# VectorE takes over GpSimd's arithmetic in the fast matrix products of a hybrid encoder layer

## The chip, the core and the metric

The kernel runs on one core of a Trainium2 chip. The core has a matrix engine (TensorE, PE in the profile), three engines for elementwise work (VectorE is DVE, ScalarE is ACT, GpSimd is POOL), SBUF for tiles of 128 partitions, and PSUM, where TensorE writes and from which VectorE and ScalarE read. All DMAs of this kernel are issued from one queue, SyncE's (SP). The metric is the time of one execution on the device in microseconds; smaller is better.

## What is computed

One layer of a residual block, 1024 real tokens and 16 meta tokens, width 1024. Two mixers (a gated delta rule and a stick-breaking attention) work on one input projection; their outputs are projected, gated, merged and projected again, and a SwiGLU feed-forward network (FFN) follows. All of it is float32. The part that matters here, shortened:

```python
D_MODEL, SEQ, D_FF = 1024, 1024, 2816
def hybrid_mixer(hn, ..., w_branch_dn, w_branch_sb, w_out):
    ...                                   # o_dn: T x 2048, o_sb: T x 1024
    merged = jax.nn.sigmoid(gate_dn) * (o_dn @ w_branch_dn) + jax.nn.sigmoid(gate_sb) * (o_sb @ w_branch_sb)
    return merged @ w_out
def swiglu(hn, w_ffn_in, w_ffn_out):
    gate, up = jnp.split(hn @ w_ffn_in, 2, axis=-1)
    return (jax.nn.silu(gate) * up) @ w_ffn_out
# per layer
h = h + hybrid_mixer(rmsnorm(h, norm_mix_gain[l]), ...)
h = h + swiglu(rmsnorm(h, norm_ffn_gain[l]), w_ffn_in[l], w_ffn_out[l])
```

## The kernel before

**Precision.** A float32 operand is cut into a high part (ScalarE casts it to the matrix engine's format) and a low part (a subtraction, the source minus the high part), and each product is three matmuls: high with high, high with low, low with high. The cut of an activation block is `split2` (tiles `b` and `t`, two casts and two subtractions of 128x1024 for a block); the cut of a weight is `w_split` (tile `ws`, one cast and one subtraction of 128x512).

**The fast product.** From the second half of the branch projection on, matrix products are done two by two blocks at a time in the Strassen-Winograd way: seven block products in place of eight, paid for with additions of operand blocks and of results. `wino_steps` does one: `A` holds the weight quadrants (tiles `w`, `wr`, `s`, `stg`), `B` the activation quadrants (`x`, `b`, `b11r`, `mg`). It issues the products in the order 1, 2, 6, 7, 4, 5, 3. `stage` runs one product as four quarters `p`; a quarter is one `w_split`, twelve matmuls of 128x512 (nine in the last group of the FFN) into one PSUM bank, and an `evac` that reads the bank. `bop` adds or subtracts activation quadrants, `aop` weight quadrants, two instructions of 128x1024 each. Of ten such pairs, five are given the engine `gx`, which is GpSimd; the others run on VectorE.

**Where it runs.** In this order: the second half of the delta-rule branch (evacuation `accumulate` into `mg`, and `gate_dn`, which multiplies by a gate tile `gt`); the stick-breaking branch (`sb_evac`, which adds gated results to `mg`); the output projection (`accumulate` into `h2`, with `h2_final` summing squares into `ssq` for the norm); and, after the first FFN projection, three groups of the second FFN projection (`accumulate` into `h3`, tile `h` in the trace). Between them lies the first FFN projection, 22 steps of `ffn_a` (two products with `b11`, `b21`) and `ffn_b` (five products with `t1`, `t2`, `b22`, `t3`, `t4`, with weight sums made by `comb` on GpSimd). Its entry norms the four quadrants and makes t1, t2, t3, t4 and b22 out of them (`each`); from tile `rows`, a ScalarE copy of the norm's PSUM row, GpSimd scales quadrant 22. Products 5 and 6 of `ffn_b` use different PSUM banks (`pb`, `pa`), and a ScalarE copy of each follows.

**What sets the order.** Tile pools hand out buffers and semaphores order their reuse. Each engine runs its own instructions strictly in the order in which the program has them, and waits at the first one that isn't ready. The order here is made when the program is built, by a scheduler that goes by a timeline of its own, so that moving an instruction to another engine, or writing it elsewhere, also moves others. All elementwise helpers (`sub`, `add`, `mul`) have one line each, L1116, L1119 and L1122; rows are told apart by the tiles.

Of the kernel before, what the change touches and what calls it, by code (L numbers as in the profile page):

```python
# [9 lines left out]
F32 = mybir.dt.float32  # L10
# [5 lines left out]
P = 128  # L16
# [24 lines left out]
def build(tc, ctx, hT, w_mix, w_ab, w_bd, w_bs, w_o, w_fi, w_fo, small, adt, outT):  # L41
    nc = tc.nc
# [1075 lines left out]
    def add(out, a, b, eng=None):  # L1118
        (eng or nc.vector).tensor_tensor(out, a, b, op=ALU.add)  # L1119

    def mul(out, a, b, eng=None):
        (eng or nc.vector).tensor_tensor(out, a, b, op=ALU.mult)  # L1122
# [5 lines left out]
    def ent(ts, k):  # L1128
        return ts[k // 2][:, k % 2]
# [21 lines left out]
    def w_split(src):  # L1151

        n = src.shape[1]
        wsn[0] += 1
        t = wp.tile([P, KT, P], R32, tag=("wh", "wl")[wsn[0] % 2], name="ws")
        hi, lo_ = t[:, 0:n], t[:, 4:4 + n]
        nc.scalar.copy(hi, src)  # L1157
        sub(lo_, src, hi.bitcast(F32))
        return hi, lo_

    def mmw(ps, w, b, kh, more=False):

        n = 3 * kh
        i = 0
        for k in range(kh):
            bh, bl = (t[:, k % 2] for t in b[k // 2])
            for (x, y) in ((w[0][:, k], bh), (w[0][:, k], bl), (w[1][:, k], bh)):
                nc.tensor.matmul(ps, x, y, start=(i == 0 and not more), stop=(i == n - 1),  # L1168
                                 skip_group_check=more)
                i += 1  # L1170
# [74 lines left out]
    def wino_steps(kh, B, A, evac, s2=None):  # L1245

        gx = nc.gpsimd
        X, Y = {}, {}  # L1250

        def stage(name, ws, b, acc, more=False):
            for p in range(4):
                w = w_split(ent(ws, p)[:, 0:kh * P].rearrange("p (k c) -> p k c", c=P))
                if not more:
                    acc[p] = bank("pa" if acc is X else "pb", p)
                mmw(acc[p], w, b, kh, more)
                evac(name, p, acc[p])

        def bop(f, o, a, b, eng=None):  # L1260
            for i in range(2):
                n = min(2, kh - 2 * i)
                f(B[o][i][:, :n], B[a][i][:, :n], B[b][i][:, :n], eng)

        def aop(f, o, a, b, eng=None):
            for x, y, z in zip(o, a, b):
                f(x[:, :, 0:kh * P], y[:, :, 0:kh * P], z[:, :, 0:kh * P], eng)

        b11 = split_of(B["11"], kh, "b")
        stage("1", A["11"], b11, X)  # L1270
        yield
        b21 = split_of(B["21"], kh, "b")
        stage("2", A["12"], b21, Y)
        yield
        bop(sub, "11", "12", "11")
        bop(sub, "11", "22", "11")
        t2 = split_of(B["11"], kh, "b")
        s2 = s2 or [wp.tile([P, KT, P], F32, tag="wr", name="s2").rearrange("p (a k) c -> p a (k c)", a=2)
              for i in range(2)]
        aop(sub, A["11"], A["11"], A["21"], gx)  # L1280
        aop(sub, s2, A["22"], A["11"])
        stage("6", s2, t2, X, True)
        bop(sub, "21", "21", "11", gx)
        bop(sub, "12", "22", "12", gx)
        bop(sub, "11", "22", "11")
        aop(add, A["21"], A["21"], A["22"], gx)
        aop(sub, A["12"], A["12"], s2, gx)
        t3 = split_of(B["12"], kh, "b")
        stage("7", A["11"], t3, X, True)
        t4 = split_of(B["21"], kh, "b")  # L1290
        stage("4", A["22"], t4, X, True)
        t1 = split_of(B["11"], kh, "b")
        b22 = split_of(B["22"], kh, "b")
        stage("5", A["21"], t1, Y)
        stage("3", A["12"], b22, Y, True)
# [21 lines left out]
    def gate(j, q, p):  # L1317
        r, hs = quad(q)
        g_ = late["g"]()
        nc.sync.dma_start(g_, gate_d[j * KT + r + p, :, hs])  # L1320
        return g_

    def gate_dn(q, p):
        c = ent(mg[q], p)
        mul(c, c, gate(0, q, p), nc.gpsimd if q == "21" else None)

    def sb_evac(u):

        v = []

        def gated(q, p, t, eng=None):
            mul(t, t, gate(1, q, p), eng)
            c = ent(mg[q], p)
            add(c, c, t, nc.gpsimd)

        def tmp():
            return late["g"]()

        def evac(name, p, ps):
            up = ent(u, p)  # L1340
            if name == "1":
                nc.scalar.copy(up, ps)
            elif name == "2":
                t = tmp()
                add(t, up, ps)
                gated("11", p, t)
            elif name == "6":
                nc.scalar.copy(up, ps)
            elif name == "7":
                if p % 2 == 0:  # L1350
                    v.append(v4(wp.tile([P, KT, P], F32, tag="wr", name="v").rearrange("p k c -> p (k c)")))
                nc.scalar.copy(ent(v, p), ps)
            elif name == "4":
                t = gate(1, "21", p)
                mul(t, t, ps)
                c = ent(mg["21"], p)
                add(c, c, t, nc.gpsimd)
            elif name == "5":
                add(ent(v, p), ent(v, p), ps)
                gated("22", p, ent(v, p))  # L1360
            else:
                add(up, up, ps)
                gated("12", p, up)

        return evac
# [41 lines left out]
    lh, lh_st = pool("lh", 1)  # L1407
    ssq = [lh.tile([P, 512], F32, name=f"ssq{i}") for i in range(2)]
    started = [False, False]
    h2 = {}  # L1410
# [7 lines left out]
    def h2_final(q, p):  # L1418
        r, hs = quad(q)
        i = int(q[1]) - 1  # L1420
        c = ent(h2[q], p)
        nc.sync.dma_start(h2_d[r + p, :, hs], c)
        if not started[i]:
            started[i] = True
            nc.scalar.activation(ssq[i], c, AF.Square)
        else:
            sq = lh.tile([P, 512], F32, name="sq2", bufs=1)
            nc.scalar.activation(sq, c, AF.Square)
            add(ssq[i], ssq[i], sq, nc.vector if p == 3 and q != "11" else nc.gpsimd)

    def norm2_sum(i):
        pss = bank(("pa", "pb")[i])
# [37 lines left out]
    def product(w, b, tag="pb"):  # L1470
        ps = bank(tag)
        mmw(ps, w, b, 4)
        return ps
# [29 lines left out]
    def ffn_b(f):  # L1503
        raw, ac, px = fst.pop(f)
        rg, ru = raw or raw_pair(f)
        h0, h1 = HS

        def comb(op, a, b):
            r = fw.tile([P, 4, P], F32, tag="sc", name="sc", bufs=3)
            nc.gpsimd.tensor_tensor(r, a, b, op=op)  # L1510
            return r

        def gate(hs, v):
            nc.scalar.activation(v, ac[:, hs], AF.Sigmoid)
            mul(ac[:, hs], ac[:, hs], v)

        a11, a12, a21, a22 = rg[:, 0:4], rg[:, 4:8], ru[:, 0:4], ru[:, 4:8]
        s1 = comb(ALU.add, a21, a22)
        w5 = w_split(s1)
        s2 = comb(ALU.subtract, s1, a11)  # L1520
        w6 = w_split(s2)
        s4 = comb(ALU.subtract, a12, s2)
        w3 = w_split(s4)
        yield
        u, v, v2 = uv[0][:, f % 2], uv[1][:, 0], uv[1][:, 1]
        gate(h0, v)
        mmw(px, w6, t2, 4, True)
        nc.scalar.copy(u, px)
        py = product(w5, t1)
        nc.scalar.copy(v, py)  # L1530
        mmw(py, w3, b22, 4, True)
        add(ac[:, h1], u, py)
        gate(h1, v2)
        s3 = comb(ALU.subtract, a11, a21)
        mmw(px, w_split(s3), t3, 4, True)
        add(v, v, px)
        mul(ac[:, h1], ac[:, h1], v)
        mmw(px, w_split(a22), t4, 4, True)
        mul(ac[:, h0], ac[:, h0], px)
        nc.sync.dma_start(act_d[f], ac)  # L1540
# [3 lines left out]
    t1, t2 = sblock(slab, "t1"), sblock(slab, "t2")  # L1544
# [1 line left out]
    r2 = norm2_sum(1)  # L1546
    ffn_a(1)
    row = norm2_row(r2, 1)
    rows = lh.tile([P, 512], F32, name="rows")
    nc.scalar.copy(rows, row)  # L1550
    norm2_scale("12", row)


    def each(f, o, a, b, dst, eng=None):
        for i in range(2):
            if f:
                f(h2[o][i], h2[a][i], h2[b][i], eng)
            split2(dst, i, h2[o][i], eng)

    each(sub, "11", "12", "11", t1)  # L1560
    for k in range(4):
        mul(ent(h2["22"], k), ent(h2["22"], k), rows, nc.gpsimd)
    for f in range(2, LEAD):
        ffn_a(f)
    for st in (lh_st, lp_st):
# [2 lines left out]
    b22, t3, t4 = sblock(sl3, "b22"), sblock(sl3, "t3"), sblock(sl3, "t4")  # L1568
    fb = ffn_b(0)
    next(fb)  # L1570

    each(None, "22", None, None, b22, nc.gpsimd)
    each(sub, "11", "22", "11", t2)
    each(sub, "21", "21", "11", t4)
    each(sub, "12", "22", "12", t3, nc.gpsimd)
    uv = [xt(4), xt(5)]

    XW = (-1, -1)
# [106 lines left out]
```

## Time and profile before

| | us |
|---|---|
| time, median of 3 runs | 2661.07 (2660.76 to 2661.66) |
| the profiled execution, its own time | 2659.11 |
| its span | 2657.4 |
| TensorE busy | 2538.1 (96%) |
| VectorE busy | 1637.1 (62%) |
| ScalarE busy | 1085.6 (41%) |
| GpSimd busy | 611.7 (23%) |

Busy shares are means over stages that differ. The changed code runs from about 1655 us to the end of the span, and in it stretches in which TensorE never stops stand beside stretches in which it waits; so the trace is read stretch by stretch. A row of the timeline gives the start, the time that the instruction took, and in brackets how long its engine stood idle before it and what released it. Two instructions of one engine overlap by some 0.07 us, so the cost of one on a full engine is the step from its start to the next one's, a little less than its duration.

### The profile page before, as it was taken

How to read it: one execution, taken by the hardware profiler on the slowest of the kernel's cores; microseconds unless marked ns; L12 is line 12 of the kernel's file. 1: busy time of each engine (PE TensorE's matmuls, PEld its weight loads, DVE VectorE, ACT ScalarE, POOL GpSimd, SP SyncE). 2: the span in 40 equal slices, each digit the busy share in tenths (PEclk: the TensorE clock that was granted, in tenths of full speed). 3: DMA queues.
4: the chain of work that ended last, by engine and by line, in shares of the span. 5: the costliest groups of instructions: out<-in, count | busy, mean ns of one | idle time of the engine just before them, and what ended most of it. 6: DMA issues, size and time to landing. Idle time of an engine off the chain costs nothing.

```text
span 2657.4 us, 40031 instructions
## 1 busy us (share of the span) xinstructions
PE 2538.1 (96%) x15877; PEld 2167.3 (82%) x15877; DVE 1637.1 (62%) x2481; ACT 1085.6 (41%) x2195; POOL 611.7 (23%) x649
## 2 busy tenths in 40 slices
PE   8999999999999999999999999879887999997999
PEld 5788887899999998999989988668676888885777
DVE  5356555346665664455545554997977555557997
ACT  5454444233333333454544554334343333342332
POOL 4011110000111111111111110444545333235221
PEclk9999999999999999999999999999997999998999
DMA  3373554532233332212121133435122222225321
GB/s 107 106 182 123 145 177 131 147 94 76 94 104 104 102 106 72 68 33 64 33 69 59 49 124 103 155 106 174 52 75 95 103 88 81 79 86 176 111 87 64
DMA packets 136440, 265.97 MB, mean 100 GB/s; under 512 B 11564, under 2 KB 55100, under 8 KB 135228
## 3 DMA queue, kind: packets, MB, share of 16 engines
q1 hardware_dynamic: 136252, 263.40, 31.3%
q8 instruction: 125, 2.05, 0.3%
q14 instruction: 63, 0.52, 0.1%
HBM read 196.50 MB, written 66.86 MB: 99 GB/s over the span
## 4 chain that ended last, share of the span: by engine, by line
PE 78%; DVE 12%; DMA 4%; issue 4%; ACT 2%; POOL 1%; SPq 0%; DVEq 0%; ACTq 0%; POOLq 0%
PE pj L108 35%; PE pa L1168 15%; PE pb L1168 10%; DVE b L1116 2%; DVE ws L1116 2%; PE pch L108 2%; DMA zs_d<-gt 2%; PE pout L1083 2%; PE ptr L1068 1%; DVE x L1116 1%; PE pout L765 1%; PE pch L754 1%; PE pout L766 1%; PE pch L760 1%; PE ptr L705 1%
## 5 line engine op out<-in xcount | busy, mean ns | idle before, releaser
L108 PE MATMUL pj<-xh,wh 128*128 128x512 f32 (+5 forms) x1600 | 579.2, 362 | 6.6 <-DVE gt L802 4.8
L108 PE MATMUL pj<-xh,wl 128*128 128x512 f32 (+5 forms) x1600 | 575.8, 360 | 0.0
L108 PE MATMUL pj<-xl,wh 128*128 128x512 f32 (+5 forms) x1600 | 571.4, 357 | 0.6 <-issue 0.6
L108 PEld LDWEIGHTS pj<-xh,wh 128*128 128x128 f32 x1600 | 303.7, 190 | 42.6 <-issue 5.4
L108 PEld LDWEIGHTS pj<-xh,wl 128*128 128x128 f32 x1600 | 303.7, 190 | 29.8 <-issue 1.0
L108 PEld LDWEIGHTS pj<-xl,wh 128*128 128x128 f32 x1600 | 304.0, 190 | 27.6
L1168 PE MATMUL pa<-b,ws 128*128 128x512 f32 x1176 | 287.6, 401 | 34.2 <-DVE h L1119 17.1
L1168 PE MATMUL pb<-b,ws 128*128 128x512 f32 x1212 | 298.4, 397 | 10.3 <-DVE ws L1116 7.7
L1168 PEld LDWEIGHTS pa<-b,ws 128*128 128x128 f32 x1176 | 224.2, 192 | 91.2 <-issue 26.6
L1168 PEld LDWEIGHTS pb<-b,ws 128*128 128x128 f32 x1212 | 229.1, 190 | 66.3 <-DVE ws L1116 11.1
L1168 PE MATMUL pa<-t,ws 128*128 128x512 f32 x792 | 195.3, 396 | 11.9 <-DVE t L1116 11.3
L1168 PEld LDWEIGHTS pa<-t,ws 128*128 128x128 f32 x792 | 150.4, 190 | 47.1 <-DVE t L1116 12.7
L296 DVE SCALAR_TENSOR_TENSOR y<-pj,sm,y 128x346 f32<-128x346 f32 (+2 forms) x216 | 119.1, 572 | 28.5 <-ACT y L292 26.1
L1116 DVE TENSOR_TENSOR ws<-wr,ws 128x512 fp32r<-128x512 f32 x90 | 80.2, 892 | 66.4 <-ACT ws L1157 66.4
L1059 DVE TENSOR_TENSOR_SCAN kpt<-kpt 128x144 f32<-128x144 f32 (+3 forms) x64 | 89.0, 1391 | 49.3 <-POOL kpt L1056 48.4
L921 DVE TENSOR_TENSOR wtl<-ptr,wth 128x512 fp32r<-128x512 f32 (+2 forms) x96 | 52.2, 552 | 101.8 <-ACT wth L920 101.6
L1510 POOL TENSOR_TENSOR sc<-wr 128x512 f32<-128x512 f32 x44 | 67.4, 1532 | 176.9 <-DVE ws L1116 170.8
L1157 ACT CAST ws<-sc 128x512 fp32r<-128x512 f32 x88 | 52.9, 620 | 123.6 <-PE pa L1168 108.9
L1054 POOL TENSOR_SCALAR_AFFINE_SELECT spt<-spt 128x128 f32<-128x128 f32 x64 | 26.7, 417 | 274.0 <-ACT spt L1051 262.7
L800 ACT ACTIVATE gt<-pj 128x512 f32<-128x512 f32 x48 | 28.6, 596 | 144.2 <-PE pj L108 97.8
L100 DVE TENSOR_TENSOR wl<-wr,wh 128x1024 fp32r<-128x1024 f32 x46 | 56.3, 1223 | 47.8 <-ACT wh L99 47.8
L108 PE MATMUL pj<-wh,xh 128*128 128x256 f32 (+1 forms) x288 | 83.7, 291 | 0.0
(431 smaller groups left out, 5028.9 us busy)
## 6 DMA issues: line engine op xcount, KB each, us to landing
wr<-in_w_mix_dram SPq DMA_DIRECT2D x80, 512.0 KB
wr<-in_w_fi_dram SPq DMA_DIRECT2D x48, 512.0 KB
act_d<-ac SPq DMA_DIRECT2D x22, 512.0 KB
lrep<-ld SPq DMA_DIRECT2D x64, 144.0 KB
zs_d<-gt SPq DMA_DIRECT2D x32, 256.0 KB
gate_d<-gt SPq DMA_DIRECT2D x32, 256.0 KB
zt<-zs_d SPq DMA_DIRECT2D x32, 256.0 KB
odn_d<-zt SPq DMA_DIRECT2D x32, 256.0 KB
```

Source lines behind the costliest of these rows:

```text
L100: (eng or nc.vector).tensor_tensor(wl, wr, wh.bitcast(F32), op=ALU.subtract)
L108: nc.tensor.matmul(ps, u, v, start=(i == 0), stop=(i == n - 1))
L296: nc.vector.scalar_tensor_tensor(y[:, oo:e], ps[:, oo - s - sh:n - sh], cw[:, m, j:j + 1], y[:, oo:e], op0=ALU.mult, op1=ALU.add)
L800: nc.scalar.activation(gt, ps, AF.Sigmoid)
L921: nc.vector.tensor_tensor(dst_l, src, dst_h.bitcast(F32), op=ALU.subtract)
L1054: nc.gpsimd.affine_select(out=spt[:, dg], in_=spt[:, dg], pattern=[[-1, P]], compare_op=ALU.is_gt, fill=0.0, base=0, channel_multiplier=1)
L1059: nc.vector.tensor_tensor_scan(out=kpt[:, 0:K][:, ::-1], data0=kpt[:, 0:K][:, ::-1], data1=kpt[:, 0:K][:, ::-1], initial=1.0, op0=ALU.mult ...
L1083: nc.tensor.matmul(po[:, 0:256], u[:, b, :], v[:, b].rearrange("p a b -> p (a b)"), start=False, stop=False)
L1116: (eng or nc.vector).tensor_tensor(out, a, b, op=ALU.subtract)
L1157: nc.scalar.copy(hi, src)
L1168: nc.tensor.matmul(ps, x, y, start=(i == 0 and not more), stop=(i == n - 1), skip_group_check=more)
L1510: nc.gpsimd.tensor_tensor(r, a, b, op=op)
```

## The change

GpSimd is left with no arithmetic in the fast products and none in the FFN's entry: `gx` becomes `None` (VectorE), the adds of `sb_evac`, the multiplications of `gate_dn` and the sums of squares go to VectorE, and so do the scaling of quadrant 22, which now reads the norm's row in PSUM and needs no copy `rows`, and the cuts of b22 and t3. The weight sums (`comb`) of the FFN's steps stay on GpSimd. In `each` the order of the cuts becomes t1, t2, b22, t3, t4, and in `ffn_b` product 5 and its copy are written ahead of product 6. As built, 101 instructions leave GpSimd for VectorE: 58 of 128x1024, 6 of 128x768, 37 of 128x512.

```diff
-        gx = nc.gpsimd
+        gx = None
...
     def gate_dn(q, p):
         c = ent(mg[q], p)
-        mul(c, c, gate(0, q, p), nc.gpsimd if q == "21" else None)
+        mul(c, c, gate(0, q, p))
...
-            add(c, c, t, nc.gpsimd)
+            add(c, c, t)
...
-            add(ssq[i], ssq[i], sq, nc.vector if p == 3 and q != "11" else nc.gpsimd)
+            add(ssq[i], ssq[i], sq)
...
         gate(h0, v)
+        py = product(w5, t1)
+        nc.scalar.copy(v, py)
         mmw(px, w6, t2, 4, True)
         nc.scalar.copy(u, px)
-        py = product(w5, t1)
-        nc.scalar.copy(v, py)
         mmw(py, w3, b22, 4, True)
...
     row = norm2_row(r2, 1)
-    rows = lh.tile([P, 512], F32, name="rows")
-    nc.scalar.copy(rows, row)
     norm2_scale("12", row)
...
-        mul(ent(h2["22"], k), ent(h2["22"], k), rows, nc.gpsimd)
+        mul(ent(h2["22"], k), ent(h2["22"], k), row)
...
-    each(None, "22", None, None, b22, nc.gpsimd)
     each(sub, "11", "22", "11", t2)
+    each(None, "22", None, None, b22)
+    each(sub, "12", "22", "12", t3)
     each(sub, "21", "21", "11", t4)
-    each(sub, "12", "22", "12", t3, nc.gpsimd)
```

**Place 1, VectorE at the end of the delta-rule branch.** `mg` with `ptr` or `pch` is an evacuation of that branch's last product, `mg` with `gt` a gate multiplication, `ws` a weight's cut, `b_177..` the cut of an activation block of the next branch, `w` and `s` weight sums of the next branch. Before:

```order
L1119 TENSOR_TENSOR mg_15872<-mg_15872,ptr 128x512
L1116 TENSOR_TENSOR ws<-w,ws 128x512
L1122 TENSOR_TENSOR mg_15872<-mg_15872,gt 128x512
L1119 TENSOR_TENSOR mg_15873<-mg_15873,pch 128x512
L1116 TENSOR_TENSOR ws<-w,ws 128x512
L1122 TENSOR_TENSOR mg_15872<-mg_15872,gt 128x512
L1116 TENSOR_TENSOR b_17741<-x,b_17740 128x1024
L1119 TENSOR_TENSOR mg_15873<-mg_15873,pch 128x512
L1116 TENSOR_TENSOR b_17743<-x,b_17742 128x1024
L1116 TENSOR_TENSOR ws<-w,ws 128x512
L1116 TENSOR_TENSOR s_17660<-w 128x1024
L1122 TENSOR_TENSOR mg_15873<-mg_15873,gt 128x512 x2
```

and now:

```order
L1116 TENSOR_TENSOR x<-x 128x1024
L1122 TENSOR_TENSOR mg_15872<-mg_15872,gt 128x512
L1119 TENSOR_TENSOR mg_15872<-mg_15872,ptr 128x512
L1116 TENSOR_TENSOR x<-x 128x1024
L1116 TENSOR_TENSOR ws<-w,ws 128x512
L1116 TENSOR_TENSOR b_17741<-x,b_17740 128x1024
L1119 TENSOR_TENSOR mg_15873<-mg_15873,pch 128x512
L1122 TENSOR_TENSOR mg_15877<-mg_15877,gt 128x512
L1116 TENSOR_TENSOR b_17743<-x,b_17742 128x1024
L1116 TENSOR_TENSOR ws<-w,ws 128x512
L1122 TENSOR_TENSOR mg_15873<-mg_15873,gt 128x512
L1116 TENSOR_TENSOR w<-w 128x1024 x2
```

Two sums `x<-x` stand there now that GpSimd did; two gate multiplications and the weight sums `w<-w` follow behind the last evacuation (`mg_15873` with `pch`).

**Place 2, VectorE in the FFN's entry,** from the scaling of quadrant 12 (L1449) on. `t_18758` and `t_18760` are the low parts of t1, the `b_189..` those of b22, `x<-x` a difference of quadrants, `ws<-sc` the cut of a weight sum. Before:

```order
L1449 SCALAR_TENSOR_TENSOR x<-x,sm,pb 128x512 x4
L1116 TENSOR_TENSOR x<-x 128x1024
L1116 TENSOR_TENSOR ws<-sc,ws 128x512
L1119 TENSOR_TENSOR ac<-ac,pb 128x512
L1116 TENSOR_TENSOR x<-x 128x1024
L1119 TENSOR_TENSOR ac<-ac,pb 128x512
L1116 TENSOR_TENSOR t_18758<-x,t_18757 128x1024
L1116 TENSOR_TENSOR x<-x 128x1024
L1116 TENSOR_TENSOR t_18760<-x,t_18759 128x1024
L1116 TENSOR_TENSOR x<-x 128x1024
L1116 TENSOR_TENSOR ws<-sc,ws 128x512
```

and now:

```order
L1449 SCALAR_TENSOR_TENSOR x<-x,sm,pb 128x512 x4
L1122 TENSOR_TENSOR x<-x,pb 128x512 x4
L1116 TENSOR_TENSOR x<-x 128x1024
L1116 TENSOR_TENSOR ws<-sc,ws 128x512
L1119 TENSOR_TENSOR ac<-ac,pb 128x512
L1116 TENSOR_TENSOR x<-x 128x1024
L1116 TENSOR_TENSOR ws<-sc,ws 128x512
L1116 TENSOR_TENSOR b_18946<-x,b_18945 128x1024
L1119 TENSOR_TENSOR ac<-ac,pb 128x512
L1116 TENSOR_TENSOR ws<-sc,ws 128x512
L1116 TENSOR_TENSOR x<-x 128x1024
L1116 TENSOR_TENSOR b_18948<-x,b_18947 128x1024
```

The four multiplications `x<-x,pb` and the cuts of b22 came over from GpSimd, ahead of the first cut of t1.

**Place 3, the start of the second FFN projection.** `x` and `b_21812` to `b_21817` are activation quadrants just loaded (`b_21810` to `b_21815` in the changed program), `s_218..` weight sums, `h` with `pa` the first evacuations. GpSimd, before:

```order
L1116 TENSOR_TENSOR x<-x 128x1024 x2
L1116 TENSOR_TENSOR b_21812<-b_21816,b_21812 128x1024
L1116 TENSOR_TENSOR b_21813<-b_21817,b_21813 128x1024
L1116 TENSOR_TENSOR x<-x 128x1024 x2
L1119 TENSOR_TENSOR x<-x,b_21818 128x1024
L1119 TENSOR_TENSOR x<-x,b_21819 128x1024
L1116 TENSOR_TENSOR wr<-wr,s_21828 128x1024
L1116 TENSOR_TENSOR wr<-wr,s_21829 128x1024
```

VectorE, before:

```order
L1116 TENSOR_TENSOR x<-b_21816,x 128x1024
L1116 TENSOR_TENSOR x<-b_21817,x 128x1024
L1116 TENSOR_TENSOR b_22003<-x,b_22002 128x1024
L1116 TENSOR_TENSOR s_21828<-b_21818,x 128x1024
L1116 TENSOR_TENSOR b_22005<-x,b_22004 128x1024
L1116 TENSOR_TENSOR s_21829<-b_21819,x 128x1024
L1116 TENSOR_TENSOR b_22089<-b_21812,b_22088 128x1024
L1119 TENSOR_TENSOR h_21830<-h_21830,pa 128x512 x2
L1116 TENSOR_TENSOR b_22091<-b_21813,b_22090 128x1024
L1116 TENSOR_TENSOR ws<-s_21828,ws 128x512
```

VectorE, now:

```order
L1116 TENSOR_TENSOR b_21810<-b_21814,b_21810 128x1024
L1116 TENSOR_TENSOR x<-b_21815,x 128x1024
L1116 TENSOR_TENSOR b_21811<-b_21815,b_21811 128x1024
L1116 TENSOR_TENSOR x<-x 128x1024
L1116 TENSOR_TENSOR b_22001<-x,b_22000 128x1024
L1116 TENSOR_TENSOR s_21826<-b_21816,x 128x1024
L1119 TENSOR_TENSOR x<-x,b_21816 128x1024
L1116 TENSOR_TENSOR x<-x 128x1024
L1116 TENSOR_TENSOR s_21827<-b_21817,x 128x1024
L1119 TENSOR_TENSOR x<-x,b_21817 128x1024
L1116 TENSOR_TENSOR b_22003<-x,b_22002 128x1024
L1119 TENSOR_TENSOR h_21828<-h_21828,pa 128x512 x2
```

GpSimd's instructions now stand between VectorE's own, ahead of the first evacuation.

## Rows read from the trace of the kernel before

**Rows 1.** Busy time by stretch: stretch, length, PE, PEld, DVE, ACT, POOL, PEclk, DMA, GB/s

```profile
1655.00:1690.00 35.00, 33.01 (x142) 26.28 (x142) 28.37 (x24) 10.40 (x14) 22.47 (x8) 1.00 0.57 212
1690.00:1778.40 88.40, 67.55 (x279) 52.27 (x277) 86.33 (x88) 29.25 (x39) 31.45 (x13) 0.96 0.40 125
1778.40:1857.40 79.00, 78.96 (x336) 64.14 (x337) 63.39 (x69) 32.61 (x49) 35.68 (x19) 0.98 0.52 161
1857.40:1910.00 52.60, 40.25 (x150) 29.59 (x149) 52.60 (x37) 19.32 (x27) 36.12 (x15) 0.90 0.11 41
...
1953.40:2016.00 62.60, 40.80 (x151) 29.49 (x150) 54.98 (x43) 24.24 (x34) 41.85 (x19) 0.74 0.21 71
2016.00:2395.00 379.00, 379.00 (x1641) 309.44 (x1640) 208.55 (x279) 139.71 (x238) 121.83 (x83) 0.99 0.26 91
...
2436.80:2457.00 20.20, 2.06 (x5) 1.18 (x5) 20.20 (x10) 6.92 (x9) 18.45 (x6) 0.59 0.54 195
2457.00:2540.00 83.00, 80.44 (x334) 63.46 (x334) 83.00 (x85) 32.32 (x43) 26.30 (x10) 0.98 0.32 102
2540.00:2657.40 117.40, 113.69 (x491) 91.95 (x490) 92.61 (x125) 38.11 (x62) 19.85 (x10) 1.00 0.24 77
```

**Rows 2.** Timeline of TensorE: waits at five places

```profile
1778.44 12.80 PE L1168 MATMUL pa<-b,ws 128*128 128x512 f32 x48 [8.71 <-DVE mg L1119]
...
1909.54 15.73 PE L1168 MATMUL pa<-b,ws 128*128 128x512 f32 x67 [0.64 <-DVE ws L1116]
...
2001.35 2.93 PE L1168 MATMUL pa<-t,ws 128*128 128x512 f32 x6 [7.53 <-DVE t L1116]
...
2015.40 5.36 PE L1168 MATMUL pb<-b,ws 128*128 128x512 f32 x12 [2.49 <-ACT x L1530]
...
2453.77 2.05 PE L1168 MATMUL pa<-b,ws 128*128 128x512 f32 x4 [17.05 <-DVE h L1119]
2456.98 23.24 PE L1168 MATMUL pa<-b,ws 128*128 128x512 f32 x92 [1.17 <-DVE ws L1116]
```

**Rows 3.** Timeline of VectorE, with GpSimd idle

```profile
1697.44 1.21 DVE L1116 TENSOR_TENSOR b<-x,b 128x1024 fp32r<-128x1024 f32 x1
1698.58 1.21 DVE L1116 TENSOR_TENSOR b11r<-x,b11r 128x1024 f32<-128x1024 f32 x1
```

**Rows 4.** Timelines of GpSimd (first row) and VectorE around 1771

```profile
1770.59 2.67 POOL L1116 TENSOR_TENSOR w<-w 128x1024 f32<-128x1024 f32 x1 [13.63 <-issue]
...
1770.98 0.67 DVE L1119 TENSOR_TENSOR mg<-mg,pch 128x512 f32<-128x512 f32 x1
1771.58 2.23 DVE L1116 TENSOR_TENSOR ws<-w,ws 128x512 fp32r<-128x512 f32 x1
```

**Rows 5.** Timelines of GpSimd (first row) and VectorE, start of the second FFN projection

```profile
2435.46 6.61 POOL L1116 TENSOR_TENSOR x<-x 128x1024 f32<-128x1024 f32 x2
...
2426.73 2.56 DVE L1116 TENSOR_TENSOR x<-b,x 128x1024 f32<-128x1024 f32 x2 [2.14 <-DMA b<-act_d]
...
2436.50 3.38 DVE L1116 TENSOR_TENSOR b<-x,b 128x1024 fp32r<-128x1024 f32 x1
...
2456.25 0.68 DVE L1116 TENSOR_TENSOR ws<-s,ws 128x512 fp32r<-128x512 f32 x1
```

**Rows 6.** Timeline of VectorE: delta-rule branch, first sum and last evacuation

```profile
1661.76 1.22 DVE L1116 TENSOR_TENSOR b11r<-x,b11r 128x1024 f32<-128x1024 f32 x1 [0.74 <-DMA x<-odn_d]
...
1777.62 0.68 DVE L1119 TENSOR_TENSOR mg<-mg,pch 128x512 f32<-128x512 f32 x1
```

**Rows 7.** Timeline of VectorE: first evacuation of the stick-breaking branch's last product

```profile
1849.45 0.69 DVE L1119 TENSOR_TENSOR u<-u,pb 128x512 f32<-128x512 f32 x1 [0.59 <-PE pb L1168]
```

**Rows 8.** Timelines of VectorE and (second row) GpSimd in the FFN's entry

```profile
1975.31 2.73 DVE L1449 SCALAR_TENSOR_TENSOR x<-x,sm,pb 128x512 f32<-128x512 f32 x4 [2.96 <-ACT rows L1550]
...
1975.55 1.30 POOL L1510 TENSOR_TENSOR sc<-wr 128x512 f32<-128x512 f32 x1 [6.16 <-DMA wr<-in_w_fi_dram]
...
2006.73 1.21 DVE L1116 TENSOR_TENSOR t<-x,t 128x1024 fp32r<-128x1024 f32 x1
```

More of the change, by code (lines that the diff above doesn't have):

```diff
@@ L1356, in evac @@
                 c = ent(mg["21"], p)
-                add(c, c, t, nc.gpsimd)
+                add(c, c, t)
             elif name == "5":
```

## The prediction

> **What bounds the kernel now.** I read the table by stretch first [rows 1]. Over the changed part TensorE is the busiest engine, but not all the time. In the FFN's steps it never stops (379.00 of 379.00 us, 1641 matmuls, 0.231 us each), in the stick-breaking branch neither (78.96 of 79.00). It stands still 20.9 us in the delta-rule branch (88.40 less 67.55), 12.4 at the start of the output projection, 21.8 in the FFN's entry, 18.1 at the start of the second FFN projection, 2.6 in the stretch after it: 75.8 us. In four of these five VectorE is full: 86.33 of 88.40, 52.60 of 52.60, 20.20 of 20.20, 83.00 of 83.00; in the entry it is at 54.98 of 62.60. The mean share of VectorE (62%) hides that. The rows of TensorE's waits say the same: what releases it is an evacuation, a weight's cut or an activation's cut on VectorE, except for one ScalarE copy [rows 2].
>
> Then: what is VectorE full of? With GpSimd idle, a 128x1024 instruction costs 1.14 us from start to start [rows 3] and a 128x512 one 0.60 (1770.98 to 1771.58) [rows 4]. The 37 instructions of the third troubled row, 1857.40 to 1910.00, are 14 of the large and 23 of the small kind, so they need 16.0 + 13.8 = 29.8 us; they took 52.60. The difference is GpSimd: while it works, an instruction of VectorE with both inputs in SBUF doesn't advance. The weight's cut at 1771.58 took 2.23 us and ended at 1773.81, 0.55 after GpSimd's sum (1770.59 to 1773.26); the one ahead of it, which reads PSUM, took its usual 0.67 under the same sum [rows 4]. Where both engines have such work ready they take turns, 3.3 us for a pair: two of GpSimd in 6.61 us, one of VectorE in 3.38 [rows 5]. In 1857.40 to 1910.00 it is 22.8 us lost to 15 instructions of GpSimd, 1.5 us each [rows 1], and each would cost VectorE 1.14 or 0.60 if it did it itself.
>
> **The change part by part.** In all 101 instructions move. At 1.14 and 0.60, with the six of 128x768 at some 0.87 (estimated between the two by size), they add 66 + 5 + 22 = 93 us to VectorE. What that is worth is decided in each stretch by what TensorE waits for there.
>
> *Delta-rule branch.* TensorE starts the next branch when the last evacuation has left the old PSUM pool: it waits 8.71 us and starts at 1778.44 [rows 2]. From the first sum at 1661.76 to that evacuation, which ends at 1778.30, VectorE takes 116.5 us [rows 6]. In the changed order the same stretch of VectorE's queue, from the same sum to the same evacuation, has 46 large and 75 small instructions: 52.4 + 45.0 = 97.4 us, ending at 1759.2. TensorE's own work from 1655 is 33.01 + 67.55 = 100.6 us [rows 1], to 1755.6, so VectorE still ends last. Gain 19.2 at most; VectorE stood idle 2.1 us here before, waiting for others, and I keep that: **17**. Two of the weight sums of the next branch and two gate multiplications now come behind the evacuation; that branch has VectorE busy 63.39 of 79.00, of which, by the same count of kinds, 47 is work and 16 is blocking [rows 1], and takes 14 us of moved adds and 7 of these with 11 to spare. The sums of TensorE are not touched there: **0**. If that cover were gone it would cost those 7. The loads don't move against VectorE's rows by more than a place or two in SP's queue: still gate tiles between weights, which wait for the gate multiplications.
>
> *Output projection.* From the first evacuation of the last product before it (1849.45) [rows 7] to its fourth product (1909.54) [rows 2] are 60.1 us, in which TensorE has 180 matmuls, 41.6 us. The changed queue from that evacuation to the first cut of the fourth product's weight has 24 large and 38 small ones: 27.4 + 22.8 = 50.2 us. VectorE still ends last, 9.9 sooner. The last cuts there are a chain of subtraction, ScalarE cast and subtraction, of which the count holds only VectorE's part, so I take 3 off: **7**.
>
> *FFN entry.* From the scaling of quadrant 12 (1975.31) to the end of the last cut of t2 (2006.73 + 1.14) VectorE takes 32.6 us [rows 8]. The changed queue has 4 scalings of 0.68, 16 large, 11 small between the two: 27.5. But weight sums of the FFN's steps stay on GpSimd, 1.30 us each [rows 8], and three of them fall in here: 31.4, gain 1.2. The cuts of b22 and the multiplications now stand ahead of t1, so the wait for t1 grows while that for t2 shrinks, and the sum counts to t2. After it TensorE waits 2.49 us for ScalarE's copy of product 5 and then takes 5.36 us for 12 matmuls [rows 2], where 12 x 0.231 are 2.8. In the changed order products 6 and 7 stand between product 5 and its bank's next use, so 2.49 goes, and most of the 2.6 with it: **6**, between 0 and 11. In the steady steps the scheduler already had product 5 ahead of 6, so that edit is worth nothing there, and the dropped copy `rows` nothing either.
>
> *Start of the second FFN projection.* From its first subtraction (2426.73, which waits for a load) to the first cut of product 6's weight (2456.25 + 0.68), for which TensorE waits at 2456.98, are 30.2 us [rows 2, 5]. The changed queue has 18 large and 6 small ones: 20.5 + 3.6 = 24.1. **6**. In the next stretch 2.6 us of waits [rows 1] are mostly GpSimd's blocking: **2**. In the last one VectorE has 24.8 us idle [rows 1] for ten moved instructions: **0**.
>
> Sum: 17 + 7 + 6 + 6 + 2 = 38. The profiled execution took 2659.11 us; 38 less is 2621.1. The median of the runs lies 1.96 above that execution, so the forecast is **2623**. [...] At the good ends (19 + 10 + 11 + 6 + 3 = 49, and 4 of the clock) it is 2608. At the bad ends, where each queue of VectorE waits for ScalarE and TensorE between its instructions as a full count doesn't (8 + 2 + 0 + 4 + 0 = 14, rounded up to 16 by the clock), it is 2645.
>
> **The rivals.**
>
> *Half of it comes back as waits inside VectorE's queue.* One queue now holds everything in order. A cut behind a sum whose load or cast is late waits with it, where GpSimd would have waited alone. For it: one such wait on a load stands in front of the second FFN projection (2.14 us) [rows 5]. Against it: in full stretches VectorE had at most 2.1 idle us in 88. About 20 us of gain: 2641.
>
> *Slower: the load goes onto the full engine and its blocking doesn't leave.* If the lengthened instructions are not GpSimd's doing, or the weight sums that stay keep it up, then VectorE gets the moved work on top where it has no idle time. In the four full stretches and the entry GpSimd's moved work is 8 large and 4 small, 9 and 5, 6 and 6, 6, and 10: 39 x 1.14 + 15 x 0.60 = 53 us, and TensorE waits for VectorE there: 2714. It decides where an instruction of GpSimd blocks VectorE for less than VectorE's own time, 0.93 us on the mean of the 101; 1.5 was found. [...]
>
> *No change.* The waits go to what comes next, the loads: the first subtraction of the second FFN projection waits for one already [rows 5], and if loads came last at all five places the time stays at 2661. Against it: of TensorE's five largest waits none was released by a load [rows 2].
>
> **How the numbers follow.** Forecast (2608 to 2634) 0.62; half of it (2634 to 2652) 0.22; better than 2608 0.03; no change 0.06; slower 0.07. A measurement of this kernel can tell about 0.2%, 5.3 us, from no change. Faster 0.87, same 0.06, slower 0.07. The range 2608 to 2645 holds the forecast and most of the second case, about 8 in 10.
>
> **What would show it.** GpSimd without work from the branch to the entry and after the FFN's steps; VectorE's 128x512 cuts at 0.68 us there without exception; the last evacuation of the delta-rule branch near 1760, TensorE's two waits at the start of the second FFN projection at 12 us together in place of 17.05 + 1.17; VectorE busy less in 1857 to 1910's counterpart in spite of more instructions. Wrong would be the forecast if VectorE shows idle time inside those queues, or if its lone instructions still take over 2 us where GpSimd is idle.

## The result and the profile after

The changed kernel takes 2611.69 us (median of 4 runs, 2607.87 to 2614.26) against 2660.91 (4 runs, 2658.07 to 2661.66): 49.2 us less, ratio 0.9822 [0.9811, 0.9834]. The forecast was 2623, 38 us less; the range 2608 to 2645 holds the time. The profiled execution of the kernel after took 2613.56 us, its span is 2611.8, so by the two profiles the gain is 45.6 us. One execution of a variant below (v1_comb) took 8762.52 us, with TensorE busy 8737.0 us in place of 2533.4; nothing is concluded from it.

Line 1 of the page after:

```profile
PE 2533.4 (97%) x15877; PEld 2168.7 (83%) x15877; DVE 1601.2 (61%) x2582; ACT 1086.0 (42%) x2194; POOL 369.2 (14%) x548
```

VectorE has 101 instructions more and is busy 35.9 us less; GpSimd is busy 242.5 us less. That points to GpSimd as what made VectorE's rows long before; the experiments test it. The tile `ws` (the cuts of weights, always 128x512, always two inputs in SBUF) shows it, after the change without exception; from the branch to the FFN's entry, before and then after, with minimum, median and longest in ns:

```profile
L1116 DVE TENSOR_TENSOR ws<-w,ws x68: 674/691/2899, 1679.7 to 1944.3; 128x512 fp32r<-128x512 f32 x68
L1116 DVE TENSOR_TENSOR ws<-s,ws x8: 678/1037/2509, 1795.5 to 1900.9; 128x512 fp32r<-128x512 f32 x8
```

```profile
L1116 DVE TENSOR_TENSOR ws<-w,ws x68: 678/684/693, 1680.6 to 1919.8; 128x512 fp32r<-128x512 f32 x68
L1116 DVE TENSOR_TENSOR ws<-s,ws x8: 683/686/692, 1780.9 to 1871.1; 128x512 fp32r<-128x512 f32 x8
```

To see where the time went, both traces are cut at the same places of the program, which differ from the round cuts of [rows 1]: the first sum of the delta-rule branch to TensorE's start in the next branch; the first evacuation of that branch's last product to the output projection's fourth product (182 and 183 matmuls on); the scaling of quadrant 12 to the point from which TensorE runs unbroken; the first subtraction of the second FFN projection to its product 6; from there to the end. Columns as in [rows 1]; before, then after:

```profile
1661.76:1778.44 116.68, 93.80 (x391) 73.13 (x389) 111.15 (x106) 37.98 (x50) 53.92 (x20) 0.97 0.42 136
...
1849.45:1909.54 60.09, 47.74 (x182) 35.58 (x180) 58.39 (x45) 20.92 (x30) 41.91 (x18) 0.91 0.12 44
...
1975.31:2015.40 40.09, 18.42 (x49) 11.59 (x47) 39.98 (x25) 15.37 (x19) 35.95 (x16) 0.60 0.12 39
...
2426.73:2456.98 30.25, 12.03 (x48) 8.89 (x46) 30.14 (x15) 8.78 (x11) 25.70 (x8) 0.72 0.71 261
2456.98:2657.40 200.42, 194.14 (x824) 155.43 (x824) 175.63 (x209) 70.42 (x104) 46.15 (x20) 0.99 0.27 87
```

```profile
1664.79:1763.60 98.81, 92.44 (x390) 73.45 (x388) 97.87 (x122) 38.12 (x50) 0.00 (x0) 0.98 0.47 156
...
1834.75:1885.20 50.45, 45.63 (x183) 35.20 (x182) 50.42 (x63) 19.07 (x27) 0.00 (x0) 0.93 0.16 53
...
1949.54:1983.30 33.76, 16.18 (x49) 11.04 (x47) 33.68 (x34) 14.44 (x18) 11.53 (x7) 0.70 0.21 65
...
2392.31:2416.92 24.61, 14.70 (x54) 10.58 (x53) 24.36 (x25) 9.93 (x12) 0.00 (x0) 0.76 0.95 347
2416.92:2611.80 194.88, 191.01 (x820) 154.34 (x820) 165.49 (x227) 69.48 (x103) 0.00 (x0) 1.00 0.27 87
```

In each stretch VectorE does more instructions (122 for 106, 63 for 45, 34 for 25, 25 for 15, 227 for 209) in less time, and in the first four it is still full: it idles 0.94, 0.03, 0.08 and 0.25 us there. So VectorE still sets the ends of the first, third and fourth, as the prediction said. In the output projection it no longer quite does: TensorE's last wait for it ends at 1877.61, before the fourth product, and TensorE reaches that product (1885.20) without another. The timeline of TensorE after, at the places of [rows 2]:

```profile
1763.62 12.82 PE L1168 MATMUL pa<-b,ws 128*128 128x512 f32 x48 [3.47 <-DVE mg L1119]
...
1877.61 2.93 PE L1168 MATMUL pa<-b,ws 128*128 128x512 f32 x6 [1.73 <-DVE b L1116]
...
1966.76 5.17 PE L1168 MATMUL pb<-t,ws 128*128 128x512 f32 x11 [9.03 <-DVE t L1116]
...
1978.13 4.49 PE L1168 MATMUL pa<-t,ws 128*128 128x512 f32 x11 [3.56 <-DVE t L1116]
1983.30 3.02 PE L1168 MATMUL pa<-t,ws 128*128 128x512 f32 x12 [0.68 <-ACT x L1530]
...
2410.07 2.04 PE L1168 MATMUL pa<-b,ws 128*128 128x512 f32 x4 [7.15 <-DVE h L1119]
2414.68 2.04 PE L1168 MATMUL pa<-b,ws 128*128 128x512 f32 x4 [2.56 <-DVE h L1119]
2416.92 10.35 PE L1168 MATMUL pa<-b,ws 128*128 128x512 f32 x40 [0.20 <-DVE ws L1116]
```

The releasers are the same evacuations and cuts on VectorE. 8.71 became 3.47; 17.05 + 1.17 became 7.15 + 2.56 + 0.20. The entry's wait of 2.49 for ScalarE's copy of product 5, out of `pb`, is gone; the 0.68 is a wait for the copy of product 6, out of `pa`, which was as long before:

```profile
2011.17 0.79 PE L1168 MATMUL pa<-t,ws 128*128 128x512 f32 x1 [0.68 <-ACT x L1528]
```

And VectorE's own rows, answering [rows 6] and [rows 4]:

```profile
1664.79 1.23 DVE L1116 TENSOR_TENSOR b11r<-x,b11r 128x1024 f32<-128x1024 f32 x1 [0.82 <-DMA x<-odn_d]
...
1762.89 0.68 DVE L1119 TENSOR_TENSOR mg<-mg,pch 128x512 f32<-128x512 f32 x1
...
1773.85 0.68 DVE L1116 TENSOR_TENSOR ws<-w,ws 128x512 fp32r<-128x512 f32 x1
```

From the start of the first sum to the end of the last evacuation are 98.8 us, where the count of the prediction had 97.4 and the kernel before 116.5.

### The profile page after: what moved, and what is told of

It reads as the page before. It is cut to its first block, busy times and chain, and to the rows that moved or that the text cites. A ratio compares the mean times of both kernels' runs of the same rounds, so it can differ in the third digit from the quotient of the medians.

```text
span 2611.8 us, 39910 instructions
## 1 busy us (share of the span) xinstructions
PE 2533.4 (97%) x15877; PEld 2168.7 (83%) x15877; DVE 1601.2 (61%) x2582; ACT 1086.0 (42%) x2194; POOL 369.2 (14%) x548
## 4 chain that ended last, share of the span: by engine, by line
PE 82%; DVE 9%; issue 3%; DMA 3%; ACT 2%; POOL 1%; SPq 0%; DVEq 0%; ACTq 0%; POOLq 0%
PE pj L108 36%; PE pa L1168 17%; PE pb L1168 12%; PE pch L108 2%; PE pout L1083 2%; PE ptr L1068 1%; DVE b L1116 1%; PE pch L754 1%; DVE x L1116 1%; PE pj L1168 1%; PE pout L765 1%; PE pout L766 1%; PE pch L760 1%; PE ptr L705 1%; DVE yk L296 1%
## 5 line engine op out<-in xcount | busy, mean ns | idle before, releaser
L1059 DVE TENSOR_TENSOR_SCAN kpt<-kpt 128x144 f32<-128x144 f32 (+3 forms) x64 | 89.0, 1391 | 50.3 <-POOL kpt L1056 49.4
L921 DVE TENSOR_TENSOR wtl<-ptr,wth 128x512 fp32r<-128x512 f32 (+2 forms) x96 | 52.2, 552 | 105.6 <-ACT wth L920 105.6
L1157 ACT CAST ws<-wr 128x512 fp32r<-128x512 f32 x90 | 55.9, 622 | 64.3 <-PE pb L1168 45.4
```

Source lines behind the costliest of these rows:

```text
L921: nc.vector.tensor_tensor(dst_l, src, dst_h.bitcast(F32), op=ALU.subtract)
L1059: nc.vector.tensor_tensor_scan(out=kpt[:, 0:K][:, ::-1], data0=kpt[:, 0:K][:, ::-1], data1=kpt[:, 0:K][:, ::-1], initial=1.0, op0=ALU.mult ...
```

## The experiments

A table first, since every kernel below is read from it. It gives the lengths of five stretches, worked out from the starts of six instructions in the timeline of VectorE: A, first sum of the delta-rule branch to its last evacuation; B, on to the first evacuation of the stick-breaking branch's last product; C, on to the scaling of quadrant 12 (the output projection is in it); D, on to the first subtraction of the second FFN projection (entry and steps of the FFN); E, on to the end of the span. The first column is where A starts. Starts and lengths are those of one profiled execution of each kernel, "time" is the median of its executions.

| kernel | A starts | A | B | C | D | E | time |
|---|---|---|---|---|---|---|---|
| before | 1661.8 | 115.9 | 71.8 | 125.9 | 451.4 | 230.7 | 2660.9 |
| after | 1664.8 | 98.1 | 71.9 | 114.8 | 442.8 | 219.5 | 2611.7 |
| e1_sums | 1661.6 | 99.9 | 73.2 | 117.1 | 449.2 | 219.4 | 2622.3 |
| e2_but_sums | 1666.9 | 113.8 | 72.8 | 122.3 | 444.3 | 231.6 | 2646.8 |
| e4_entry | 1661.0 | 115.9 | 71.9 | 125.2 | 443.3 | 231.7 | 2650.6 |
| e3_old_order | 1661.1 | 98.2 | 72.2 | 115.0 | 443.0 | 219.6 | 2610.0 |
| e5_cuts_back | 1661.9 | 98.1 | 72.3 | 115.0 | 451.1 | 220.6 | 2622.7 |
| m1_read | 1659.6 | 105.6 | 81.8 | 119.0 | 442.9 | 229.7 | 2642.6 |
| m2_memset | 1664.3 | 98.2 | 78.6 | 114.8 | 443.6 | 219.2 | 2618.1 |
| v3_b22_later | 1658.5 | 98.3 | 72.1 | 114.9 | 443.4 | 219.5 | 2610.6 |
| v1b_comb | 1658.1 | 98.2 | 72.2 | 114.9 | 443.4 | 219.2 | 2607.9 |

Untouched stretches repeat within 1.4 us from kernel to kernel (A in the five with the same work in it: 98.1 to 98.3; E in the same five: 219.2 to 220.6). What varies is the start of A, 1658.1 to 1666.9, ahead of which nothing was changed. So a stretch can tell a difference of some 1.4 us, and the whole time only a larger one: the kernel before had a median of 2660.91 beside the kernel after, 2657.78 beside the runs named e1 to e4, 2657.31 beside m1, m2, v1_comb and v3, and 2659.33 beside e5 and v1b, up to 3.6 us apart.

**The sums alone** (before with one line changed):

```diff
-        gx = nc.gpsimd
+        gx = None
```

> The kernel before with one line changed: the sums of operands in the branches and projections (the variable gx) go to VectorE; gate multiplications, adds of the gated products, sums of squares and the FFN's entry stay on GpSimd. Theory (GpSimd blocks VectorE's two-input instructions; the place where VectorE is full gives the gain): the delta-rule branch gives some 14 of the 17.9 us that the whole change gave there (four small instructions of GpSimd stay, 1.5 less 0.6 each), the output projection 8 of 11, the second FFN projection 11 of 11, the FFN's entry 0: about 33 us, 2628. Rival (the gain needs GpSimd wholly free of arithmetic, since what stays still locks in turns with VectorE): under 20 us, above 2641.

Measured: 2622.26 (ratio 0.9869 [0.9855, 0.9884]), 35.5 less than the kernel before: A 16.0 of the 17.8 that the whole change gave, C 8.7 of 11.1, D 2.3 of 8.7, E 11.3 of 11.2; B loses 1.3. The 33 hold, and the rival (under 20) falls. The 2.3 in D, in whose entry no sum of the `gx` kind stands, were not expected. 2.1 of it lie in the entry, in the wait of 2.49 for ScalarE's copy and the 12 matmuls behind it (5.36 before):

```profile
1990.82 4.33 PE L1168 MATMUL pb<-b,ws 128*128 128x512 f32 x12 [1.41 <-ACT x L1530]
```

The cut and the multiplication of VectorE that this copy waits for took 1.21 and 2.84 us there, 3.39 and 1.75 in the kernel before: GpSimd's work in the entry was the same, but fell otherwise beside them.

**All but the sums** (after, with `gx = nc.gpsimd`):

> The kernel after with gx back on GpSimd: the rest of the change alone. Theory: what the first run leaves of the whole, 49 less 33 = 16 us, of which the FFN's entry is 8 to 9: about 2645. If the parts need each other, this run and the first one sum to clearly less than 49; if they share one cover, to more.

Measured: 2646.77 (0.9968 [0.9955, 0.9981]), 11.0 less than the kernel before and less than the 16 expected. D gives 7.2, C 3.6, A 2.0; B and E each lose 0.9, no more than such stretches vary. With the first run it is 46.5 of 49.2: the parts add up, within what the whole time can tell.

**The FFN's entry alone** (before, with the last three pieces of the diff and the order of products 5 and 6):

> The kernel before with the FFN's entry alone changed (the scaling of quadrant 22, the cuts of b22 and t3 on VectorE, their order, no copy rows, product 5 ahead of 6). Theory: 8.7 us as in the trace of the kernel after from the scaling of quadrant 12 to the second FFN projection, 2652. Rival (the entry's gain came from the sums of squares no longer on GpSimd ahead of it): under 4 us.

Measured: 2650.61 (0.9975 [0.9965, 0.9985]). D is 8.1 shorter, against 8.7; the rival (under 4) falls, and the sums of squares, which stay on GpSimd here, have at most 0.6 of it, less than a stretch can tell.

**The old order of products 5 and 6** (after):

```diff
-        py = product(w5, t1)
-        nc.scalar.copy(v, py)
         mmw(px, w6, t2, 4, True)
         nc.scalar.copy(u, px)
+        py = product(w5, t1)
+        nc.scalar.copy(v, py)
```

> The kernel after with product 6 ahead of 5 in the FFN's steps again. Theory of the prediction: in the steady steps nothing; in the entry the 2.5 us wait for ScalarE's copy of product 5 returns, and with it up to 2.6 us of slow TensorE clock: 2614 to 2617, 2.5 to 5 us above the kernel after. Rival (the wait only moved to the activation's cuts): no difference, 2612.

Measured: 2609.97 (0.9819 [0.9799, 0.9839]); D is 443.0 against 442.8. Nothing of the 2.5 to 5 us comes back, and with it the prediction's reason for the wait of 2.49 falls. As built, TensorE's queue with the old order differs by two places where two matmuls change with two others, and VectorE's not at all; product 5 goes first with either. What made ScalarE's copy late stands in the trace of before, ScalarE's row last:

```profile
2009.67 3.39 DVE L1116 TENSOR_TENSOR t<-x,t 128x1024 fp32r<-128x1024 f32 x1
2012.98 1.75 DVE L1122 TENSOR_TENSOR ac<-ac,x 128x512 f32<-128x512 f32 x1
...
2014.76 0.59 ACT L1530 COPY x<-pb 128x512 f32<-128x512 f32 x1 [3.13 <-DVE ac L1122]
```

The copy writes the tile that the gate's multiplication on VectorE reads, and waited 3.13 us for it. The multiplication took 1.75 in place of 0.6, behind a cut of 3.39 in place of 1.14. So it was blocking once more; the edit of the order has no part in it. In the kernel after, 12 matmuls into `pa` also stand ahead of the next use of `pb`, whichever order is written; what they hide of the wait was not measured apart.

**Cuts of b22 and t3 back on GpSimd** (after):

```diff
-    each(None, "22", None, None, b22)
-    each(sub, "12", "22", "12", t3)
+    each(None, "22", None, None, b22, nc.gpsimd)
+    each(sub, "12", "22", "12", t3, nc.gpsimd)
```

> The kernel after with b22's two cuts, t3's two sums and t3's two cuts back on GpSimd, in the new order of the cuts; six instructions of 128x1024. Theory (in the entry, too, a GpSimd instruction costs VectorE 1.5 to 2.2 us where its own would cost 1.14): the stretch from the scaling of quadrant 12 to the second FFN projection, 442.8 us in the kernel after, gets longer by 2 to 6.5 us; whole time 2614 to 2618. Rival (the entry's 8.7 us came from the scaling of quadrant 22, read from PSUM without a copy, and from the order of the cuts): the stretch stays within 1 us of 442.8, 2612.

Measured: 2622.72 (0.9869 [0.9851, 0.9888]), D 451.1: 8.3 longer, more than the 6.5 at the upper end, and about the length of before (451.4). So these six instructions account for the whole of the entry's gain, 1.4 us each on the path. 5.6 of the 8.3 come up to the point from which TensorE runs unbroken (39.37 us from the scaling of quadrant 12, for 33.76); that is 0.9 for each of the six above VectorE's own time, as expected. The other 2.7 come behind it: in the next 10 us TensorE does 37 matmuls, the first 7 of them in 3.35 us, where the kernel after does 44, all at a granted clock of 1.00, and later waits 0.81 for a ScalarE copy. Timelines of its entry, GpSimd, VectorE and TensorE:

```profile
1952.72 3.10 POOL L1116 TENSOR_TENSOR b<-x,b 128x1024 fp32r<-128x1024 f32 x1 [0.31 <-ACT b L1140]
...
1953.54 2.84 DVE L1116 TENSOR_TENSOR ws<-sc,ws 128x512 fp32r<-128x512 f32 x1
...
1967.44 5.06 PE L1168 MATMUL pb<-t,ws 128*128 128x512 f32 x11 [11.84 <-DVE t L1116]
```

A cut of 0.68 takes 2.84 under GpSimd's of 3.10, and TensorE's wait of 9.03 grows to 11.84.

**Is it the reading, or any work of GpSimd?** Two kernels add to the kernel after work whose result nobody reads (`gx` is set there only to mark the places):

```diff
+        def dup(o):
+            for j in range(o.shape[1]):
+                o_ = o[:, j, 0:384]
+                nc.gpsimd.tensor_tensor(scr, o_, o_, op=ALU.add)
...
+                if eng:
+                    dup(B[o][i][:, :n])
```

> The kernel after with about 118 extra additions on GpSimd, each of 128x384 from SBUF into a scratch tile that nobody reads, one behind every half of a sum that the change moved to VectorE: 20 in each branch, the rest in the output projection and the second FFN projection. No engine waits for their results. By the 1.30 us of a 128x512 weight sum each takes some 1.0 us (estimate by size). Theory (a GpSimd instruction that reads SBUF stops VectorE's two-input instructions for as long as it runs): the delta-rule branch and the output projection each lose 10 to 20 us, the start of the second FFN projection some 5 to 10, the stick-breaking branch little: 2612 + 25 to 50, near 2645. Rival (VectorE lost time before only by its own and GpSimd's turns on shared buffers and semaphores): no difference from 2612.

In the second, the addition is 128x4 and three `memset` of `scr` follow it:

> The same extra work at the same places, but each extra instruction is three memsets of 128x384 into the scratch tile, behind an addition of 128x4 that ties it to the same sum: GpSimd is busy, yet reads next to nothing from SBUF. Theory (it is the reading that blocks): within 4 us of 2612. Rival (any work of GpSimd blocks VectorE): as much as the run with reads, in proportion to GpSimd's busy time.

Measured: 2642.58 (0.9946 [0.9931, 0.9961]) with reads, 2618.09 (0.9850 [0.9833, 0.9866]) with memsets, although GpSimd is busier there. Line 1 of the two pages, reads and then memsets:

```profile
PE 2538.9 (96%) x15877; PEld 2169.2 (82%) x15877; DVE 1638.5 (62%) x2582; ACT 1085.7 (41%) x2194; POOL 543.9 (21%) x666
```

```profile
PE 2533.7 (97%) x15877; PEld 2167.2 (83%) x15877; DVE 1600.7 (61%) x2582; ACT 1084.7 (41%) x2194; POOL 622.9 (24%) x1020
```

The same 2582 instructions of VectorE are busy 37.8 us longer beside the reads; beside the memsets they are as short as in the kernel after (1601.2). The reads cost A 7.5, C 4.2 and E 10.2; the memsets cost 0.1, 0.0 and -0.3. The time with reads is near the expected 2645, but not part by part: A and C were to lose 10 to 20 each, and B little. The time with memsets is 6.4 above that of the kernel after, not within 4; B, below, has the difference. In VectorE's timeline a sum under reads, and a cut under memsets, each after the GpSimd row beside it:

```profile
1784.74 9.02 POOL L1266 TENSOR_TENSOR scr<-x 128x384 f32<-128x384 f32 x8
...
1786.36 1.85 DVE L1116 TENSOR_TENSOR w<-w,s 128x1024 f32<-128x1024 f32 x1
1788.13 0.68 DVE L1119 TENSOR_TENSOR g<-u,pb 128x512 f32<-128x512 f32 x1
```

```profile
1776.00 1.37 POOL L1268 MEMSET scr<- 128x384 f32 x3
...
1775.96 1.23 DVE L1116 TENSOR_TENSOR b<-x,b 128x1024 fp32r<-128x1024 f32 x1
```

A sum with two SBUF inputs grew from 1.22 to 1.85 under the reads; the evacuation, with one input in PSUM, kept 0.68. Under a memset, which has no input, the cut with two SBUF inputs took 1.23.

Both kernels lose in B (9.9 and 6.8), and most of that has another cause: a load into a tile isn't issued before the extra reader is done, and the loads of gates stand behind it in SyncE's queue. In the kernel with memsets, SyncE's longest wait in 1740 to 1800 (total, times, longest), and what VectorE then waits for (7.93 us for such a load with reads):

```profile
SPq L1430 <- POOL scr L1266: 17.4, 4, 9.0
```

```profile
1790.92 0.69 DVE L1122 TENSOR_TENSOR g<-g 128x512 f32<-128x512 f32 x1 [8.21 <-DMA g<-gate_d]
```

The price of reading is then nearest the difference of the two, 24.5 us for 118 additions, as far as the held loads cost both the same.

**Two attempts at more.** The cuts of b22 written behind t3's:

> The kernel after with the cuts of b22 written behind t3's: in VectorE's queue they then stand behind t2's cuts. Theory (the entry is bound by VectorE's queue): the cuts of t1 and t2 come 2.3 to 3.5 us sooner (two instructions of 1.14, one of them stretched to 2.2), TensorE's waits of 9.03 and 3.56 shrink by 2 to 3 in all, 2609. Rival (TensorE then waits the same for b22): 2612.

Measured: 2610.64 (0.9825 [0.9811, 0.9840]), D 443.4: no gain, as its rival said. TensorE's timeline in the entry:

```profile
1959.01 1.22 PE L1168 MATMUL pb<-t,ws 128*128 128x512 f32 x2 [7.37 <-DVE t L1116]
...
1972.66 4.49 PE L1168 MATMUL pa<-t,ws 128*128 128x512 f32 x11 [5.54 <-DVE t L1116]
```

t1 came sooner (7.37 for 9.03), but the cuts of b22 landed between t1's and t2's, and the wait for t2 grew by a little more (5.54 for 3.56). Here, on a full engine, the order within the queue moved a wait and didn't shorten the sum.

The weight sums `comb` on VectorE too (`nc.vector.tensor_tensor(r, a, b, op=op)`):

> The kernel after with the weight sums of the FFN's steps on VectorE too, so that GpSimd does no arithmetic behind the delta-rule scan but the norm's two small ones. Theory: in the entry seven sums at 0.60 on VectorE replace some 3.4 us by which its rows there were stretched: between 1 us gained and 1 lost; the steady steps, where TensorE never stops and VectorE is busy 0.55, lose nothing although VectorE takes 80 more instructions: 2611 to 2613. Rival (one queue for everything delays the weights of a step): TensorE waits appear in the steps, some 22 x 0.5 to 1 us, 2623 to 2634.

> The kernel with the weight sums of the FFN's steps on VectorE, once more, for its trace. Its time before was 2611.88. Theory: no wait of TensorE inside the steps, the entry within 1 us of 442.8. Rival: waits of TensorE in the steps, made up for by a shorter entry.

Measured: three executions of 2609.95, 2610.76 and 2613.01 (0.9827 [0.9811, 0.9844]; the median of all four is 2611.88), and 2607.85 in the single execution of the second run, whose trace gives the stretches. D is 443.4, with no wait of TensorE inside the steps. VectorE has room there (290.47 us busy in the 443.42 of D), so 88 sums more cost nothing and bring nothing. None of these times is clear of those of the kernel after (2607.87 to 2614.26).

## Why the prediction was right, and where it was short

The five terms, forecast and measured (from the stretches above; for C its whole length):

| term | forecast | measured |
|---|---|---|
| delta-rule branch | 17 | 17.9 |
| output projection | 7 | 11.1 |
| FFN entry | 6 | 8.7 |
| start of the second FFN projection | 6 | 5.6 |
| the stretch behind it | 2 | 5.5 |

With the branch between (0 forecast, 0.1 lost) that is 48.6; the profiled execution of the kernel after began stretch A 3.0 us later than that of before, which leaves the 45.6 of the spans. The medians are 49.2 apart. That is the 49 that the prediction's good ends add up to ahead of the clock, and 3.7 us from the good end of its range. No run shows the 4 us that the range adds for the clock at its good end, or the clock's part in the 16 at its bad end; what the runs showed is a granted clock of 0.98, 0.93, 0.70 and 0.76 in the first four stretches of the profile after, for 0.97, 0.91, 0.60 and 0.72 before. Of the five terms, three were too small by 2.7 to 4.1, one by 0.9, and one was too large by 0.4.

*The method was right.* The count of VectorE's queue at the price of rows with GpSimd idle gave 97.4, 50.2 and 24.1 us for three stretches; VectorE took 98.8, 50.3 and 24.6. (The "19.2 at most" of the first is 116.5 less 97.4, 19.1.) TensorE's waits at the start of the second FFN projection, forecast at 12 together, are 10.1 (7.15 + 2.56 + 0.20 and 0.21 later). e1_sums, e5_cuts_back and the pair m1_read and m2_memset show the cause.

*Output projection: the 3 us taken off for the chain through ScalarE were wrong.* The bare count was met within 0.3: 9.6 of the 11.1 come up to the fourth product, 1.4 behind it. VectorE had other work in its queue while ScalarE cast (it is busy 50.42 of 50.45). "VectorE still ends last" held only just: VectorE's cut for the fourth product ended at 1885.04, and TensorE came to the product at 1885.20 without waiting.

*Entry: the size was short by 2.7, and a reason was wrong.* To t2's last cut 1.9 came (32.6 to 30.7) where 1.2 was forecast, although seven weight sums fell in there and not three: they lengthened VectorE's 27.5 by 3.2, less than 0.5 each, where 1.30 each was counted. From that cut to TensorE's unbroken run 7.5 became 3.0, of which only 2.49 had been counted, and on the ground of the order of products, which e3_old_order refutes: that the wait went was right by luck. The 2.3 of faster matmuls behind the wait (12 in 3.02 at a granted clock of 1.00, before in 5.36 at 0.53) were foreseen, at "most of the 2.6".

*The last stretch: 2.6 us of waits were read as 2, and 5.5 went.* Product 6 starts four matmuls further on in the kernel after, so 0.9 of the 5.5 belong to the term above it. For the rest, a short wait cost TensorE more than its length. In its own columns (length, busy, granted clock) the first 10 us behind product 6's start, before and after:

```profile
2456.98:2466.98 10.00, 10.00 (x36) 0.81 0.35 111
```

```profile
2416.92:2426.92 10.00, 10.00 (x40) 0.91 0.26 90
```

Four matmuls more in the first 10 us, at a granted clock of 0.91 for 0.81, are some 0.9 us at 0.231 each. And between 2496.98 and 2556.98 the kernel before ran 243 matmuls, where the kernel after runs 264 in as long (3 x 88):

```profile
2496.98:2516.98 20.00, 19.43 (x84) 1.00 0.09 26
2516.98:2536.98 20.00, 18.17 (x75) 1.00 0.19 54
2536.98:2556.98 20.00, 19.84 (x84) 1.00 0.43 133
```

21 of them are 4.9 us, counted in whole stretches of 20 us, though the waits in between add up to 2.6. The granted clock is 1.00 throughout. From start to start it is some 4.2: a matmul ahead of a wait counts as busy for 0.39 us, where the next one otherwise starts after 0.23, and the first behind a wait takes some 0.34 to the next start (an estimate from the row below, of the kernel before: 2.58 for ten, less eight at 0.231 and the last at 0.39):

```profile
2523.89 2.58 PE L1168 MATMUL pa<-b,ws 128*128 128x512 f32 x10 [0.19 <-DVE ws L1116]
```

*The rivals.* "Half returns as waits inside VectorE's queue" fell: VectorE idles 1.3 us in the four full stretches together, and 1.5 in the first 83 us of the last (81.53 busy of 83.00). "Slower" fell at its own condition: a GpSimd instruction that reads costs VectorE more than VectorE's own would (e5_cuts_back: for each of six 0.9 us of VectorE's queue above what VectorE itself takes, and 1.4 of path). The change turned round, from a full VectorE to GpSimd, would here cost 49 us. "No change" fell: no load ends TensorE's waits there.

## What to carry to other kernels

Where VectorE is full and GpSimd works beside it, compare the durations of one form of instruction: if its longest is several times its median (before, 2899 ns for 691 in the cuts of weights), price the queue with the shortest and count who would do GpSimd's work in how much. Look at the stretch and not at the mean share: in the entry six sums and cuts were worth 1.4 us each, in the FFN's steps 88 sums nothing. Once the queue is full of its own work only, reordering it moved waits here (v3_b22_later: 7.37 and 5.54 us for 9.03 and 3.56); what is left is less work.

## What the runs showed that was not expected

It seems that VectorE isn't always the one that is stopped. In the kernel with memsets, GpSimd's tie of 128x4, which takes as little as 0.20 us elsewhere, took 8.60 while VectorE ran nine two-input instructions in a row at their usual price; it ended as VectorE's pair at 1774.60 did:

```profile
1767.34 8.60 POOL L1266 TENSOR_TENSOR scr<-w 128x4 f32<-128x4 f32 x1 [43.28 <-DVE w L1116]
...
1784.28 0.20 POOL L1266 TENSOR_TENSOR scr<-x 128x4 f32<-128x4 f32 x1
...
1768.86 1.22 DVE L1116 TENSOR_TENSOR s<-w 128x1024 f32<-128x1024 f32 x1
...
1774.60 1.28 DVE L1116 TENSOR_TENSOR ws<-w,ws 128x512 fp32r<-128x512 f32 x2
```

In the kernel with reads four additions took 14.53 us at that place, where eight took the 9.02 shown above:

```profile
1770.13 14.53 POOL L1266 TENSOR_TENSOR scr<-w 128x384 f32<-128x384 f32 x4 [56.70 <-DVE w L1116]
```

That may be one reason why the 118 additions lengthened VectorE's work by 37.8 us and not by the 74 that their number times the 0.63 of a stretched row (1.85 less 1.22) would make; of the 37.8, 24.5 reached the whole time. GpSimd's instruction started at 1767.34, the first of VectorE's nine at 1768.25, and it ended only with the ninth. That it waited for VectorE all that time is read from these two places alone; what decides when GpSimd gets its turn was not tried and stays open.
